# Forgetting attention: the cumulated gates enter the logits by a product instead of a DMA into the keys

## The chip, the cores and the metric

One core of a Trainium2 chip runs one program. The metric is the device time of one execution in microseconds; here, the median of three runs. TensorE multiplies, VectorE and ScalarE work elementwise and reduce, GpSimd takes a part of the elementwise work, and SyncE issues most of the DMAs. Each engine works through its own instructions in order and waits on semaphores for the others.

## The reference, cut to what matters

The program computes two transformer blocks on 256 tokens of width 1024. The change lies in the first of four branches of the first block, an attention of 16 heads of 64 with forget gates. A logit of query t and key s is a scaled product plus the difference of the cumulated log gates; a softmax over the keys up to t follows.

```python
fq = rms(heads(proj("fox_q"), 16), fox_q_norm_g)
fk = rms(heads(proj("fox_k"), 16), fox_k_norm_g)
log_f = log_sigmoid(proj("fox_f") + b_forget)          # one per token and head
cum_f = cumsum(log_f, axis=-1)
logits = einsum('bhqd,bhkd->bhqk', q, k) * scale + (cum_f[..., :, None] - cum_f[..., None, :])
logits = where(k_pos <= q_pos, logits, -inf)
y = softmax(logits) @ v
```

The term of the query is the same for all keys of a row, so the softmax removes it; only minus cum_f of the key is needed.

## The kernel before, in words

Activations lie feature by token: 8 tiles of 128 features by 256 tokens. A projection multiplies a unit of 128 x 1024 weights by the activations. To keep fp32 accuracy with the faster fp32r products, each unit and each activation is split into a high and a low part (`split`, line 357 on ScalarE for the high part, line 360 on VectorE or GpSimd for the low one), and three products of eight steps are summed (`mm3`; all products are at line 370). `unit` fetches weights by SyncE DMAs ahead of use, in one fixed order for the whole program.

`fox` is the branch of the change. It first projects the 16 forget gates (`st<-hh,wff`, 16 columns), takes their log sigmoid, and cumulates them along the tokens into `ncf`, 16 rows by 256 tokens, which holds minus cum_f with one head in each partition. Then four passes follow, each over a pair of head tiles (f and f+1, so four heads): a step for the queries, a step for the keys, a step for the values and the first two heads, and a step for the other two heads. `norm` copies a projection (`hraw`), squares it (`hsq`), sums the squares of each head by a product with a block matrix (`st<-hsq,cb`), takes the inverse root by Newton steps on VectorE (`nv`, `nr`, `nt`, 128x512 each), and scales twice. One of the scaled tiles has zeros in partitions 64 to 127 and the other in 0 to 63, since the gain is zero there (`fqg`, `fkg`), so a full product of 128 rows gives the logits of one head.

The zero half leaves a spare partition in each: 64 in the first tile, 0 in the second. Before the change it carries the gates. GpSimd writes ones into that row of the queries (line 909), and a DMA from ScalarE's queue copies the head's row of `ncf` into that row of the keys (line 915), four DMAs in a pass. The product of queries and keys then adds minus cum_f of the key by itself.

`fox_head` computes the logits of one head in a PSUM tile (`lg`): 128 queries by the first 128 keys, and the other 128 queries by all 256 keys. A VectorE instruction adds the mask and finds the maximum (line 933), ScalarE takes the exponential with its sum, VectorE divides (`fs`, line 367), TensorE transposes three tiles (`pt`, line 942), and ScalarE copies them out (`fp`). `av_pair` multiplies two heads with the values (`av`).

What sets the order: the program is written as generators. The passes of `fox` are woven one step at a time with the second branch's gated products (`branch(1, ...)`), and behind the last of them comes the next attention (`stick`). The modulation sums (`adacc`) run on VectorE as filler at a lower priority. From the written order and these priorities a planner lays down a fixed list for each engine: it simulates the engines with costs of its own, and at each point an engine takes the instruction of highest priority whose inputs are due by then. At run time each list is worked through in order. The PSUM tiles of the attention come from a pool of four, handed out in written order.

Of the kernel before, what the change touches and what calls it, by code (L numbers as in the profile page):

```python
# [18 lines left out]
P = 128  # L19
# [249 lines left out]
def flat(t):  # L269
    return t.rearrange("p f n -> p (f n)")  # L270
# [51 lines left out]
class Builder:  # L322
# [339 lines left out]
    def block1(self, xt, ct, fill):  # L662
        nc = self.nc
        with self.pool("b1") as bp, self.phase("b1t", t1=4, t2=6):
# [45 lines left out]
            yf = newy()  # L710
            fox = self.fox(h, yf, bp)
            step(fox, 3)
            weave((fox, 1), (self.branch(1, h, yl, acc, False), 1))
            ys = newy()
            stick = self.stick(h, ys, bp)
# [154 lines left out]
    def fox(self, h, y, bp):  # L870
        nc = self.nc

        ps = self.st()
        wf = self.wff
        n = 0
        for x, w in ((h[0], wf[0]), (h[1], wf[0]), (h[0], wf[1])):
            for k in range(KT):
                self.mm(ps[:16, :T], w[:, k * 16:(k + 1) * 16], x[:, k], start=n == 0, stop=n == 23)
                n += 1
        z, e = self.t("fz", rows=16), self.t("fe", rows=16)  # L880
        ncf = bp.tile([16, T], F32, tag="ncf", name="ncf")
        self.act(z, ps[:16, :T], AF.Identity, bias=self.pvc("bf")[:16])
        self.softplus_abs(e, z)

        self.ts(z, z, 0.0, None, ALU.min)
        self.tt(e, e, z, ALU.subtract)
        nc.vector.tensor_tensor_scan(out=ncf, data0=self.ones_t[:16], data1=e, initial=0.0, op0=ALU.mult,
                                     op1=ALU.add)
        cm = self.cst("cmask")
        rows = ((0, P), (P, 384))  # L890

        def norm(ps, tag, g):
            raw, sq = self.t("hraw", 512), self.t("hsq", 512)
            self.act(raw, ps)
            self.act(sq, ps, AF.Square)
            st = self.st()
            self.mm(st, self.cst("b64"), sq)
            r = self.rsqrt(st, 512, 64)
            out = [bp.tile([P, 2, T], F32, tag=f"{tag}{i}", name=f"{tag}{i}", bufs=2) for i in range(2)]
            for i in range(2):  # L900
                self.stt(flat(out[i]), raw, g[:, i:i + 1], r, ALU.mult, ALU.mult)
            return out


        spare = (64, 0)
        for f in range(0, KT, 2):
            qz = norm(self.pair("foxq", f, h), "qz", self.fqg)
            for i, row in enumerate(spare):
                nc.gpsimd.memset(qz[i][row:row + 1], 1.0)
            yield  # L910
            kz = norm(self.pair("foxk", f, h), "kz", self.pvs("fkg"))
            for i, row in enumerate(spare):
                for j in range(2):
                    hd = 2 * (f + j) + i
                    nc.scalar.dma_start(kz[i][row:row + 1, j], ncf[hd:hd + 1])
            yield
            v = bp.tile([P, 2, T], F32, tag="av", name="fv", bufs=2)
            self.act(v, self.tok("foxv", f // 2, h))
            for j in range(2):
                pts = [self.fox_head(qz[i][:, j], kz[i][:, j], cm, rows) for i in range(2)]  # L920
                self.av_pair(y, f + j, v, j, pts)
                yield

    def fox_head(self, q, k, cm, rows):
        nc = self.nc
        lg = self.ps("lg")
        self.mm(lg[:, 0:P], q[:, 0:P], k[:, 0:P])
        self.mm(lg[:, P:384], q[:, P:], k)

        s = self.t("fs", 384)  # L930
        nm, sm = self.col("fnm", 2), self.col("fsm", 2)
        for qt, (a, b) in enumerate(rows):
            nc.vector.tensor_tensor_reduce(out=s[:, a:b], in0=lg[:, a:b], in1=cm[:, T - (b - a):], scale=-1.0,
                                           scalar=3e38, op0=ALU.add, op1=ALU.min, accum_out=nm[:, qt:qt + 1])
            self.act(s[:, a:b], s[:, a:b], AF.Exp, scale=-1.0, bias=nm[:, qt:qt + 1], accum_out=sm[:, qt:qt + 1])
        nc.vector.reciprocal(sm, sm)
        pt = self.ps("pt")
        for qt, (a, b) in enumerate(rows):
            self.ts(s[:, a:b], s[:, a:b], sm[:, qt:qt + 1], None, ALU.mult)
            for j, c in enumerate(range(a, b, P)):  # L940
                o = T if j else qt * P
                nc.tensor.transpose(pt[:, o:o + P], s[:, c:c + P], self.cst("ident"))
        p = self.t("fp", 384)
        self.act(p, pt[:, :384])
        return p
# [688 lines left out]
```

## Time and profile before

| | us |
|---|---|
| median of 3 runs | 3097.9 |
| runs, lowest and highest | 3092.52 and 3099.93 |
| the profiled execution | 3095.87 |
| its span in the trace | 3094.1 |
| TensorE products busy | 2809.3 |
| VectorE busy | 2152.1 |
| ScalarE busy | 1344.0 |
| GpSimd busy | 851.9 |

The profile is of one execution. The span runs from the first to the last instruction in the trace; the 1.8 us to the profiled execution's time lie around it. PE is TensorE's products and PEld its weight loads, which lie under the products; DVE is VectorE, ACT ScalarE, POOL GpSimd and SP SyncE; ACTq is ScalarE's queue issuing a DMA. A group names what is written and what is read by the program's names, as `lg<-kz,qz` for the logits from keys and queries. "Idle before" is how long the engine did nothing ahead of an instruction, with what ended it; "issue" means that nothing the trace shows ended it.

### The profile page before, as it was taken

Reading aid. Unit: us, or ns where it says so; the run is one execution under the profiler, and the core shown is the slowest. Engines: PE = TensorE matmul, PEld = TensorE weight load, DVE = VectorE, ACT = ScalarE, POOL = GpSimd, SP = SyncE. Lnnn points to the kernel's source line nnn. Section 1 sums busy time; section 2 is a strip of 40 time slices with the busy share of each in tenths; the row PEclk is TensorE's granted clock in tenths of the full one; section 3 lists DMA queues with packets and bytes.
Section 4 is the critical chain, followed back from the end, with each engine's and each line's share of the span. In section 5 each row is a group of like instructions: output and inputs, shape, how many; then the busy total and the mean of one; then the engine's idle time right before and its main releaser. Section 6 shows DMA issues by size and latency. Waiting matters only on the chain. (4 is left out here: it accounts for less than half of the span.)

```text
span 3094.1 us, 49653 instructions
## 1 busy us (share of the span) xinstructions
PE 2809.3 (91%) x19760; PEld 2635.7 (85%) x19760; DVE 2152.1 (70%) x3412; ACT 1344.0 (43%) x2047; POOL 851.9 (28%) x643
## 2 busy tenths in 40 slices
PE   7997889988799887898999998999999999999898
PEld 6897778888799886798899988999998888888898
DVE  7599764679974899957699348868844499321554
ACT  5474446533344544345645554445434332111443
POOL 3243322243324434542102105444520111100000
PEclk9999999998899998999999999999999999999999
DMA  5345333466547555687656986654743223344353
GB/s 201 138 164 179 114 105 132 146 214 214 192 148 266 200 190 188 214 309 284 240 206 244 333 318 235 248 202 156 281 157 123 97 96 109 120 150 153 123 179 108
DMA packets 153416, 578.18 MB, mean 187 GB/s; under 512 B 17628, under 2 KB 17756, under 8 KB 146656
## 3 DMA queue, kind: packets, MB, share of 16 engines
q1 hardware_dynamic: 152496, 574.45, 52.1%
q8 instruction: 155, 2.54, 0.3%
q10 hardware_dynamic: 688, 0.56, 0.1%
q14 instruction: 77, 0.63, 0.1%
HBM read 516.73 MB, written 58.20 MB: 186 GB/s over the span
## 5 line engine op out<-in xcount | busy, mean ns | idle before, releaser
L357 ACT ACTIVATE whi<-raw 128x1024 fp32r<-128x1024 f32 (+1 forms) x650 | 675.7, 1045 | 747.4 <-PE mm L370 397.8
L360 POOL TENSOR_TENSOR wlo<-raw,whi 128x1024 fp32r<-128x1024 f32 (+1 forms) x248 | 647.0, 2613 | 1010.3 <-ACT whi L357 721.2
L360 DVE TENSOR_TENSOR wlo<-raw,whi 128x1024 fp32r<-128x1024 f32 (+1 forms) x293 | 382.8, 1307 | 242.3 <-ACT whi L357 231.0
L370 PE MATMUL mm<-hh,whi 128*128 128x256 f32 x3184 | 485.7, 294 | 33.1 <-DVE cv L360 19.2
L370 PE MATMUL mm<-hh,wlo 128*128 128x256 f32 x3184 | 469.3, 290 | 19.7 <-DVE wlo L360 17.6
L370 PE MATMUL mm<-hl,whi 128*128 128x256 f32 x3184 | 475.3, 292 | 0.0
L370 PEld LDWEIGHTS mm<-hh,whi 128*128 128x128 f32 x3184 | 431.2, 198 | 46.8 <-DVE cv L360 20.9
L370 PEld LDWEIGHTS mm<-hh,wlo 128*128 128x128 f32 x3184 | 426.0, 197 | 23.2 <-DVE wlo L360 18.8
L370 PEld LDWEIGHTS mm<-hl,whi 128*128 128x128 f32 x3184 | 431.7, 200 | 4.3 <-issue 3.6
L363 DVE SCALAR_TENSOR_TENSOR ca<-yp,pv,ca 128x256 f32<-128x256 f32 x720 | 357.2, 557 | 2.2
L370 PE MATMUL mm<-h,raw 128*128 128x256 f32 x1184 | 267.1, 379 | 0.0
L370 PEld LDWEIGHTS mm<-h,raw 128*128 128x128 f32 x1184 | 222.7, 190 | 29.5 <-issue 0.4
L363 DVE SCALAR_TENSOR_TENSOR adacc<-wada,sc,adacc 128x1024 f32<-128x1024 f32 x140 | 229.9, 1659 | 7.2 <-DMA wada<-in_wa 6.8
L360 POOL TENSOR_TENSOR gF<-cum 128x128 f32<-128x128 f32 x192 | 98.2, 542 | 337.2 <-DVE cum L1192 171.3
L370 PE MATMUL mm<-yh,whi 128*128 128x256 f32 x896 | 139.7, 295 | 23.1 <-ACT yh L357 16.3
L370 PEld LDWEIGHTS mm<-yh,whi 128*128 128x128 f32 x896 | 122.6, 199 | 30.1 <-ACT yh L357 20.6
L363 DVE SCALAR_TENSOR_TENSOR gt<-gt,mm 128x256 f32<-128x256 f32 x72 | 29.9, 416 | 161.7 <-ACT gt L357 161.6
L370 PE MATMUL mm<-yh,wlo 128*128 128x256 f32 x896 | 133.2, 290 | 2.8 <-DVE wlo L360 2.8
L370 PE MATMUL mm<-yl,whi 128*128 128x256 f32 x896 | 133.0, 290 | 2.6 <-DVE yl L363 2.1
L370 PEld LDWEIGHTS mm<-yh,wlo 128*128 128x128 f32 x896 | 120.0, 197 | 4.4 <-DVE wlo L360 3.2
L370 PEld LDWEIGHTS mm<-yl,whi 128*128 128x128 f32 x896 | 120.2, 197 | 3.6 <-DVE yl L363 2.7
L370 PE MATMUL mm<-y,raw 128*128 128x256 f32 x512 | 116.5, 384 | 0.0
(289 smaller groups left out, 4069.2 us busy)
## 6 DMA issues: line engine op xcount, KB each, us to landing
raw<-in_ws SPq DMA_DIRECT2D x744, 512.0 KB, 3.8
lo<-wlo SPq DMA_DIRECT2D x109, 512.0 KB, 3.0
wlo<-lo SPq DMA_DIRECT2D x109, 512.0 KB, 3.6
wada<-in_wa SPq DMA_DIRECT2D x48, 1024.0 KB, 4.9
raw<-in_ws SPq DMA_DIRECT2D x32, 384.0 KB, 3.0
memt<-in_tok SPq DMA_DIRECT2D x4, 256.0 KB, 4.6
xt<-in_tok SPq DMA_DIRECT2D x1, 1024.0 KB, 6.8
ct<-in_tok SPq DMA_DIRECT2D x1, 1024.0 KB
```

The costliest lines, as they stand in the source:

```text
L357: return self.nc.scalar.activation(out, in_, f, **k)
L360: return (eng or self.nc.vector).tensor_tensor(out=out, in0=a, in1=b, op=op)
L363: return self.nc.vector.scalar_tensor_tensor(out=out, in0=a, scalar=s, in1=b, op0=op0, op1=op1)
L370: return self.nc.tensor.matmul(out, lhsT=l, rhs=r, start=start, stop=stop, **k)
```

## The change

The ones row of the queries and the gate row of the keys are no longer written: the eight memsets and the sixteen DMAs are gone, and `norm`'s tiles are used as they are. `fox_head` gets `ncf` and the head's number instead. Ahead of each of its two logits products it adds one more product into the same PSUM columns: the stationary operand is the head's column of a 16 x 16 identity, repeated over 128 columns by a step of zero, and the moving operand is `ncf`, 16 rows by 128 or 256 tokens. That product writes the head's row of `ncf` to all 128 queries, and the product of queries and keys is summed on top.

```diff
--- before.py
+++ after.py
@@ -901,31 +901,27 @@
                 self.stt(flat(out[i]), raw, g[:, i:i + 1], r, ALU.mult, ALU.mult)
             return out
 
-
-        spare = (64, 0)
         for f in range(0, KT, 2):
             qz = norm(self.pair("foxq", f, h), "qz", self.fqg)
-            for i, row in enumerate(spare):
-                nc.gpsimd.memset(qz[i][row:row + 1], 1.0)
             yield
             kz = norm(self.pair("foxk", f, h), "kz", self.pvs("fkg"))
-            for i, row in enumerate(spare):
-                for j in range(2):
-                    hd = 2 * (f + j) + i
-                    nc.scalar.dma_start(kz[i][row:row + 1, j], ncf[hd:hd + 1])
             yield
             v = bp.tile([P, 2, T], F32, tag="av", name="fv", bufs=2)
             self.act(v, self.tok("foxv", f // 2, h))
             for j in range(2):
-                pts = [self.fox_head(qz[i][:, j], kz[i][:, j], cm, rows) for i in range(2)]
+                pts = [self.fox_head(qz[i][:, j], kz[i][:, j], ncf, 2 * (f + j) + i, cm, rows) for i in range(2)]
                 self.av_pair(y, f + j, v, j, pts)
                 yield
 
-    def fox_head(self, q, k, cm, rows):
+    def fox_head(self, q, k, ncf, hd, cm, rows):
         nc = self.nc
         lg = self.ps("lg")
-        self.mm(lg[:, 0:P], q[:, 0:P], k[:, 0:P])
-        self.mm(lg[:, P:384], q[:, P:], k)
+
+        pick = self.cst("ident")[:16, hd:hd + 1].to_broadcast([16, P])
+        self.mm(lg[:, 0:P], pick, ncf[:, 0:P], stop=False)
+        self.mm(lg[:, 0:P], q[:, 0:P], k[:, 0:P], start=False)
+        self.mm(lg[:, P:384], pick, ncf, stop=False)
+        self.mm(lg[:, P:384], q[:, P:], k, start=False)
 
         s = self.t("fs", 384)
         nm, sm = self.col("fnm", 2), self.col("fsm", 2)
```

## Rows read from the trace of the kernel before

**Rows 1.** The page, part 1: engine, busy us, share of the span, instructions.

```profile
PE 2809.3 (91%) x19760; PEld 2635.7 (85%) x19760; DVE 2152.1 (70%) x3412; ACT 1344.0 (43%) x2047; POOL 851.9 (28%) x643
```

**Rows 2.** Waits, 255 to 455 us: engine, line, releaser: total us, times, longest us.

```profile
PE lg L370 <- DMA kz<-ncf: 25.0, 4, 7.7
...
POOL qz L909 <- DVE qz L363: 14.0, 4, 5.8
...
PE pt L942 <- DVE fs L367: 7.7, 6, 1.8
```

**Rows 3.** Timeline, the four waits: start us, us, engine, line, instructions, [idle before].

```profile
276.16 1.42 DVE L363 SCALAR_TENSOR_TENSOR kz<-hraw,pv,nr 128x512 f32<-128x512 f32 x2
276.94 2.79 ACTq L915 DMA_DIRECT2D kz<-ncf  x4
...
280.53 1.62 PE L370 MATMUL lg<-kz,qz 128*128 128x128 f32 x4 [6.74 <-DMA kz<-ncf]
...
334.34 2.43 ACTq L915 DMA_DIRECT2D kz<-ncf  x4
...
336.61 1.62 PE L370 MATMUL lg<-kz,qz 128*128 128x128 f32 x4 [6.14 <-DMA kz<-ncf]
...
382.19 2.43 ACTq L915 DMA_DIRECT2D kz<-ncf  x4
...
383.94 1.02 PE L370 MATMUL lg<-kz,qz 128*128 128x128 f32 x4 [4.49 <-DMA kz<-ncf]
...
429.21 2.44 ACTq L915 DMA_DIRECT2D kz<-ncf  x4
...
432.45 1.62 PE L370 MATMUL lg<-kz,qz 128*128 128x128 f32 x4 [7.65 <-DMA kz<-ncf]
```

**Rows 4.** Timeline, VectorE and GpSimd ahead of the first and third wait.

```profile
255.67 1.22 DVE L360 TENSOR_TENSOR wlo<-raw,whi 128x1024 fp32r<-128x1024 f32 x1
...
260.74 3.56 DVE L363 SCALAR_TENSOR_TENSOR qz<-hraw,fqgs,nr 128x512 f32<-128x512 f32 x2
...
264.83 3.49 DVE L360 TENSOR_TENSOR wlo<-raw,whi 128x1024 fp32r<-128x1024 f32 x1
264.86 2.38 POOL L360 TENSOR_TENSOR wlo<-raw,whi 128x1024 fp32r<-128x1024 f32 x1
...
270.04 2.89 DVE L363 SCALAR_TENSOR_TENSOR nr<-nt,nr 128x512 f32<-128x512 f32 x1
...
371.34 2.78 DVE L360 TENSOR_TENSOR nt<-nr 128x512 f32<-128x512 f32 x1
...
377.35 2.88 DVE L363 SCALAR_TENSOR_TENSOR nt<-nt,nv 128x512 f32<-128x512 f32 x1
```

**Rows 5.** Groups by form, TensorE, whole span: shapes, count | busy us, mean ns | idle before.

```profile
L370 PE MATMUL mm<-h,raw 128*128 128x256 f32 x1184 | 267.1, 379 | 0.0
...
L370 PE MATMUL lg<-kz,qz 128*128 128x256 f32 x32 | 11.1, 432 | 0.0
...
L370 PE MATMUL lg<-kz,qz 128*128 128x128 f32 x32 | 7.4, 317 | 25.0 <-DMA kz<-ncf 25.0
...
L370 PE MATMUL st<-hh,wffh 128*16 128x256 f32 x8 | 1.1, 278 | 0.0
```

**Rows 6.** Timeline, TensorE, from one head to the next.

```profile
288.78 0.33 PE L942 MATMUL pt<-cc,fs 128*128 128x128 f32 x1 [0.28 <-DVE fs L367]
...
288.94 0.39 PE L370 MATMUL lg<-kz,qz 128*128 128x128 f32 x2
...
289.17 0.38 PE L942 MATMUL pt<-cc,fs 128*128 128x128 f32 x2
```

**Rows 7.** Timeline, TensorE's weight loads, after the products with the values.

```profile
292.29 0.19 PEld L370 LDWEIGHTS av<-fp,fv 128*64 128x64 f32 x2 [0.16 <-issue]
...
292.86 0.20 PEld L942 LDWEIGHTS pt<-cc,fs 128*128 128x128 f32 x2 [0.39 <-issue]
```

**Rows 8.** Windows: us, busy us (count) of PE, PEld, DVE, ACT, POOL; PEclk; DMA; GB/s.

```profile
277.00:287.00 10.00, 6.47 (x33) 6.32 (x34) 8.44 (x13) 3.10 (x6) 1.94 (x1) 0.66 0.42 148
```

## The prediction

> **What bounds the kernel now.** I read the page's busy shares first: TensorE is busy for 91% of the span [rows 1]. An engine that full sets the end, so a microsecond taken from it or given to it anywhere in the middle reaches the end, unless it was idle there. The change touches only the forgetting attention, which lies between some 240 and 460 us, so everything below is about TensorE in that stretch.
>
> The waits of the stretch come next [rows 2]. TensorE's largest is the first logits product of each pair of head tiles on the DMA that writes the gate row into the keys: four waits, 25.0 us in all. The next is 7.7 us on the softmax rows, in six waits. GpSimd loses 14.0 us ahead of the memsets of the ones row. The 25.0 us look like what the change is to gain.
>
> The timeline shows what the four waits consist of [rows 3]. In the first, VectorE starts the two key tiles at 276.16, 1.42 us for both; ScalarE issues the four DMAs from 276.94 on, for 2.79 us; the product starts at 280.53, after 6.74 us of idle time. So only the part from 276.94 on belongs to the DMA, 3.59 us, and the 3.15 us before it are a wait for VectorE that no edit of the change removes. The same difference, product start less start of the DMA issue, is 2.27, 1.75 and 3.24 us in the other three. Together the DMA has 10.85 of the 25.0 us; some 14.2 us are VectorE's.
>
> Why does TensorE arrive too early at all? The kernel's order on each engine is fixed ahead by a planner which puts an instruction where it expects its inputs. The product stands in the middle of a run of projections, which shows that it was placed by its due time. VectorE is what comes late [rows 4]. A split of a weight tile takes 1.22 us on VectorE at 255.67 and 3.49 us at 264.83, while GpSimd's split (264.86, 2.38 us) runs; two scalings of 128x512 take 3.56 us at 260.74, against 1.42 for the two of the keys in rows 3; a Newton step at 270.04 takes 2.89, against 0.71 for one of those. The excess is 2.27 + 2.14 + 2.18 = 6.6 us, and the first wait is 6.74 us. Before the third wait two steps of 2.78 and 2.88 us exceed 0.71 by 4.2 us, and that wait is 4.49 us. I read from this that the planner's place for the product is right but for the slowing of VectorE, and so that it already allows for the DMA about what the DMA takes.
>
> **The change part by part.** *DMAs and memsets go.* Sixteen DMAs of 1 KB leave ScalarE's queue and eight one-row memsets leave GpSimd. If the product kept its place among TensorE's instructions, each of the four waits would end when VectorE has written the first key tile: 10.85 us less. But the planner has no DMA to allow for any more and can put the product earlier by the same allowance. Work that stood before the product, and filled that time, then stands behind it. The period of one pair is the time from the key projection to the product, which gets shorter by the DMA, plus TensorE's work from the product to the next key projection, which gets longer by what was moved. Between the ends, 10.85 us of gain and none, I take none, by rows 4; 3 us would be what is left if the allowance were two thirds of the measured time.
>
> *The products added.* Each of 16 heads gets two: the same columns as its logits (128 and 256), with 16 rows of contraction instead of 128, and a stationary operand that repeats one column. Every fp32 product is two instructions here (64 logits instructions for 16 heads and two products) [rows 5]. A dense fp32 instruction of 256 columns costs 267.1 / 1184 = 0.226 us, and I take half, 0.113, for 128. A head costs 2 x (0.226 + 0.113) = 0.68 us, 16 heads 10.8 us. The upper end is the busy time of the present logits instructions with their tails and slow clock, 11.1 + 7.4 = 18.5 us. The lower end is the nearest row with a small operand: the forget gate's products with 16 columns, 1.1 us for eight of 256 columns, 0.14 us each with its tail; 64 instructions at half that for 32 of them make 6.7 us. I take 10.8, since the shape streamed is that of the logits. No row shows a product of 16 contraction rows. The Trainium skill ("TensorE: Matmul & The Clock Gate", section "Why this matters for your kernels") states that one matmul over 32 rows takes as long as one over 128; by it the sum would be the same 10.8 us, and no run here shows it yet.
>
> *What hides them.* Almost nothing. Heads follow each other tightly: the logits of the next head stand between the transposes of the last one (one transpose, two logits instructions, two transposes, then the rest of the logits) [rows 6]; so the next head's PSUM tile is taken only once the last head's transposes have begun, and its added products land there, in dense work. Only the first head of each pair can run its added products ahead of the keys, early, where TensorE is filled with projections too. All 10.8 us lie on TensorE's path. The logits of a head are ready 0.68 us later for VectorE, which has TensorE's projections as cover.
>
> *ScalarE and GpSimd freed.* ScalarE's next weight conversion is queued behind the four DMAs, which wait for the keys; GpSimd's next split stands behind the memsets, which wait for the scaled queries. Both start earlier. Who waits for them is TensorE's weights, and in rows 2 no wait of TensorE on them is as large as those shown. I cost this at nothing; the ends are 2.2 us of VectorE's slowing per split that moves into the key chain, 8.8 us for four, and as much of a gain where one moves out.
>
> *Clock.* After a wait TensorE runs slow: over 277 to 287 us the granted clock is 0.66 [rows 8], so part of it is at the 1.2 GHz level, after 6.74 us without work. At most 3.4 us per wait are lost so, 13.6 in all, and less, because the clock is low while there is nothing to run too. With waits as long as before it stays; I take 0, with up to half of it back where the waits shrink.
>
> The sum: 0 + 10.8 + 0 + 0 = +10.8 us on the profiled execution, 3095.9, makes 3106.7. That execution is 2.0 us below the median of the three runs, 3097.9; put on the median, the sum gives 3108.7. The forecast, between the two, is 3108.
>
> **The rivals.** *A, the waits shrink by the DMA.* The product stays where it is, 10.85 us go, the added products bring 10.8, and the sum is 0: 3096 to 3098. With half of the clock's loss back it is -6.8 us, 3091. For it: 10.85 us are measured. Against it: the planner places by due time, rows 4. It decides where the planner's allowance for the DMA is below 1 us or so.
>
> *B, TensorE empties at each change of height.* Going from 128 rows to 16 and back, the next weights aren't loaded under the running product. The row for it is the exit from the 64-column products with the values: the load of the next transpose sits idle for 0.39 us [rows 7]. Against it: the forget gate's 16-column products, eight in 1.1 us, have no such gap around them in rows 5. With two visits to the small shape per head, 32 visits at some 0.24 us (a half of 0.39, rounded up for the entry) are 7.7 us more: 3116. The upper end, 0.39 at every visit, is 12.5, 3121. The Trainium skill ("TensorEngine Tiling (Array Packing)", section "Tiling Modes", under "Key Properties") says that a change of tiling mode drains TensorE; the trace agrees for the 64-column products and not for the 16-column ones.
>
> *C, freed splits lengthen the key chain.* ScalarE converts during the chain, GpSimd splits during it, and VectorE slows four times by 2.2 us: +8.8 on top, 3117. It decides from the first GpSimd split that overlaps a Newton step of the keys more than now.
>
> *D, the new order dissolves the waits.* With other places for projections and splits TensorE has work until the keys are there: 25.0 us less, the clock's loss partly back, 10.8 more: -14 to -20, 3078 to 3084. Nothing in the profile speaks for it but that the order is made anew. That the change doesn't do what it says is no case: DMA and memsets can't remain.
>
> **How the numbers follow.** Forecast 0.42, A 0.20 (half of it with the clock back), B 0.20, C 0.10, D 0.08. What a measurement here can tell from no change is 0.3%, 9.3 us: 3088.6 to 3107.2. The forecast's own range is 3103 to 3116 by the bounds of the added products; a third of it is within 0.3%. Slower: 0.28 + 0.18 + 0.08, less a little for a gain elsewhere, 0.50. Faster: D and a part of A, 0.16. Same: the rest, 0.34. The range leaves out D and the far end of B and C: 3088 to 3121.
>
> **What would show it.** Right: the wait of TensorE at the first logits product of a pair is still there, four times, with VectorE's key tile as its releaser and together 18 to 26 us long; 64 new product instructions cost about 10 us of TensorE; the stretch from the forget gate's products to the last head ends some 10 us later. Wrong: the four waits sum to 15 us or less (A or D); loads with idle time beside the added products (B); longer waits and GpSimd splits inside the key chain (C). The prediction fails most simply if the planner allowed less for the DMA than it takes.

## The result, and the profile after

The changed kernel takes 3116.18 us (median of six runs, 3110.14 to 3123.13), before 3095.24 in runs beside it. The ratio is 1.0065, with a 95% interval of 1.0047 to 1.0083: 20 us slower. The forecast was 3108, slower by 10 to 13. The profiled execution of after took 3122.5 us, 6 us above its median, so of the difference of the two traces the last few microseconds are that execution's own.

The page, part 1, with its span:

```profile
span 3120.7 us, 49737 instructions
...
PE 2836.5 (91%) x19824; PEld 2648.1 (85%) x19824; DVE 2154.4 (69%) x3412; ACT 1342.3 (43%) x2047; POOL 841.6 (27%) x635
```

TensorE has 64 instructions more and 27.2 us more of busy time than in [rows 1]; VectorE and ScalarE have what they had. GpSimd has lost the eight memsets.

TensorE's waits in the same part of the work (255 to 480 us; columns as in [rows 2]):

```profile
PE lg L370 <- DVE kz L363: 17.7, 4, 6.0
PE pt L938 <- DVE fs L367: 5.5, 5, 1.4
PE mm L370 <- DVE wlo L360: 2.5, 1, 2.5
```

The four waits at the first logits product of a pass are still there, now for VectorE's key tile, and 17.7 us long in place of the 25.0 of [rows 2]. The timeline has them one by one, to be read beside [rows 3]:

```profile
279.76 0.80 PE L370 MATMUL lg<-kz,qz 128*128 128x128 f32 x2 [6.04 <-DVE kz L363]
280.49 1.22 PE L370 MATMUL lg<-ncf,cc 16*128 16x256 f32 x2
281.64 1.22 PE L370 MATMUL lg<-kz,qz 128*128 128x256 f32 x2
282.30 1.20 PE L370 MATMUL mm<-hh,whi 128*128 128x256 f32 x3
...
334.37 0.80 PE L370 MATMUL lg<-kz,qz 128*128 128x128 f32 x2 [3.61 <-DVE kz L363]
...
390.44 0.52 PE L370 MATMUL lg<-kz,qz 128*128 128x128 f32 x2 [2.28 <-DVE kz L363]
...
443.01 0.80 PE L370 MATMUL lg<-kz,qz 128*128 128x128 f32 x2 [5.74 <-DVE kz L363]
```

The first pass of after gets its keys 0.77 us earlier than before (279.76 against 280.53), the last 10.56 us later (443.01 against 432.45). So the loss grows pass by pass, in what TensorE does between the waits. From one head to the next, the timeline of after, to be read beside [rows 6]:

```profile
287.27 0.27 PE L938 MATMUL pt<-cc,fs 128*128 128x128 f32 x1
287.47 0.48 PE L370 MATMUL lg<-ncf,cc 16*128 16x128 f32 x2
287.88 0.44 PE L938 MATMUL pt<-cc,fs 128*128 128x128 f32 x2
288.16 0.39 PE L370 MATMUL lg<-kz,qz 128*128 128x128 f32 x2
288.47 0.69 PE L370 MATMUL lg<-ncf,cc 16*128 16x256 f32 x2
289.10 0.70 PE L370 MATMUL lg<-kz,qz 128*128 128x256 f32 x2
289.44 0.94 PE L370 MATMUL mm<-yl,whi 128*128 128x256 f32 x5
```

The same stretch of the kernel before ends here, as does the first head's:

```profile
281.59 1.63 PE L370 MATMUL mm<-hl,whi 128*128 128x256 f32 x5
...
289.63 0.94 PE L370 MATMUL mm<-hh,whi 128*128 128x256 f32 x5
```

From the first transpose to the next projection before took 289.63 - 288.78 = 0.85 us and after takes 289.44 - 287.27 = 2.17: 1.32 us more, where the prediction had 0.68. The weight loads of the same stretch show why:

```profile
287.47 0.29 PEld L370 LDWEIGHTS lg<-ncf,cc 16*128 16x128 f32 x2 [0.16 <-issue]
287.88 0.20 PEld L938 LDWEIGHTS pt<-cc,fs 128*128 128x128 f32 x2
288.05 0.30 PEld L370 LDWEIGHTS lg<-kz,qz 128*128 128x128 f32 x2
288.47 0.29 PEld L370 LDWEIGHTS lg<-ncf,cc 16*128 16x128 f32 x2
289.10 0.30 PEld L370 LDWEIGHTS lg<-kz,qz 128*128 128x128 f32 x2 [0.33 <-issue]
```

A load normally begins some 0.1 us ahead of its product, under the product before it, as at 288.05 for the product at 288.16. At each change between 16 and 128 rows, load and product begin together (287.47, 287.88, 288.47 and 289.10 in both fences), and the load sits idle before that, for up to 0.33 us. After a wait TensorE runs at the lower of its two levels, 1.2 GHz: from 443 to 447 us the granted clock is 0.50. There loads, products and the idle time before the loads are longer (the last row is that window: its us, TensorE's busy us and instructions, the granted clock, the DMA's share, GB/s):

```profile
443.74 0.50 PEld L370 LDWEIGHTS lg<-ncf,cc 16*128 16x128 f32 x2 [0.22 <-issue]
444.88 0.50 PEld L370 LDWEIGHTS lg<-kz,qz 128*128 128x128 f32 x2 [0.65 <-issue]
...
443.00:447.00 4.00, 3.99 (x12) 0.50 0.45 183
```

**The sum from the trace.** Of four heads in a pass, the first costs its early product (0.41 us) and 282.30 - 279.76 = 2.54 us, against 281.59 - 280.53 = 1.06 before: 1.9 more. Two cost 1.32 more; the one that meets the products with the values costs some 1.1 more by the same reading (in the second pass 347.69 to 351.49 us in after, 344.82 to 347.47 before). That is 4 x (1.9 + 2 x 1.32 + 1.1) = 22.6 us of products, less 7.3 us of waits: 15.3. A milestone behind the branch is the first instruction of the next attention on ScalarE, the absolute value of `z`; it begins at 457.6 us before and 474.2 after, 16.6 later. The rest arises behind that: at the first modulation sum (`adas`, 577.9 and 598.5) the distance is 20.6 us.

### The profile page after: what moved, and what is told of

The parts are those of the page before. It is cut to its first block, busy times and chain, and to the rows that moved or that the text cites. A ratio compares the mean times of both kernels' runs of the same rounds, so it can differ in the third digit from the quotient of the medians.

```text
span 3120.7 us, 49737 instructions
## 1 busy us (share of the span) xinstructions
PE 2836.5 (91%) x19824; PEld 2648.1 (85%) x19824; DVE 2154.4 (69%) x3412; ACT 1342.3 (43%) x2047; POOL 841.6 (27%) x635
## 3 DMA queue, kind: packets, MB, share of 16 engines
q8 instruction: 155, 2.54, 0.3%
## 5 line engine op out<-in xcount | busy, mean ns | idle before, releaser
L370 PEld LDWEIGHTS mm<-hh,wlo 128*128 128x128 f32 x3184 | 426.6, 197 | 22.7 <-DVE wlo L360 18.7
```

What stands on the lines that cost most here:

```text
L370: return self.nc.tensor.matmul(out, lhsT=l, rhs=r, start=start, stop=stop, **k)
```

## The experiments

Two theories of the products' price were set against each other: H, TensorE empties at each change of height between 16 and 128 rows; and O, the products cost that much by themselves. The waits were a separate question: what is the DMA's part worth, and why is VectorE late at all? "Milestone" is the first `se<-z` of each trace, 457.6 us before and 474.2 after.

**No DMA, no memsets, no products.**

```diff
-        pick = self.cst("ident")[:16, hd:hd + 1].to_broadcast([16, P])
-        self.mm(lg[:, 0:P], pick, ncf[:, 0:P], stop=False)
-        self.mm(lg[:, 0:P], q[:, 0:P], k[:, 0:P], start=False)
-        self.mm(lg[:, P:384], pick, ncf, stop=False)
-        self.mm(lg[:, P:384], q[:, P:], k, start=False)
+        self.mm(lg[:, 0:P], q[:, 0:P], k[:, 0:P])
+        self.mm(lg[:, P:384], q[:, P:], k)
```

> The changed kernel without its added products: neither DMA, memsets nor products, so the gates are left out of the logits. It measures what taking the DMA and the memsets away is worth by itself. The forecast's step (the planner moves the product up by the DMA's time) expects nothing: 3095 us, 0 against before. Rival A (the waits shrink by the DMA's 10.85 us, part of the clock's loss comes back) expects 3079 to 3084. The trace of after shows four waits of 17.7 us in place of 25.0, 7.3 us less; if that reading is whole, 3088.

Measured: 3091.31 us, 0.9985 of before (0.9972 to 0.9999), so 4.6 us less. The milestone is at 449.7, 7.8 us earlier. TensorE's waits in this kernel:

```profile
PE lg L370 <- DVE kz L363: 17.4, 4, 5.8
```

The forecast's 0 lies just outside the interval and rival A's 14 to 19 us far outside; the 7.3 us read from the trace of after lie within it. 7.6 us of waits go, the branch ends 7.8 us earlier, and 4 of these are lost again by the first `adas` (574.1 against 577.9, 3.8 earlier); "Left open" below says why. After stands 24.4 us behind this kernel there (598.5 against 574.1), which is the products' price by this pair.

**The products alone, beside the DMA.** The kernel before, with `fox_head` as after.

> The kernel before with the added products beside the DMA and the memsets, so the gates are added twice. It measures the products by themselves, with the waits of before in place. If the sum of after is two separate terms (23.2 us of products, 7.3 us of waits gone), this gives 23 us over before: 3118, above after. If the products run in the time of the waits, it is at most 3107.

Measured: 3119.06 us, 1.0074 (1.0056 to 1.0091): 23 us, as two separate terms would have it. The waits are 23.9 us long, nearly those of [rows 2], with the DMA as their releaser, so the products don't run in their time. At the first `adas` the products cost 22.5 us by this pair (600.4 against 577.9). TensorE's waits for the keys:

```profile
PE lg L370 <- DMA kz<-ncf: 23.9, 4, 10.9
```

**The products 128 rows high.**

```diff
-        ncf = bp.tile([16, T], F32, tag="ncf", name="ncf")
+        ncf = bp.tile([P, T], F32, tag="ncf", name="ncf")
+        nc.gpsimd.memset(ncf, 0.0)
...
-        pick = self.cst("ident")[:16, hd:hd + 1].to_broadcast([16, P])
+        pick = self.cst("ident")[:, hd:hd + 1].to_broadcast([P, P])
```

> The changed kernel with the added products made 128 rows high: the gates' tile has 128 partitions, zero from 16 on, and the repeated column of the identity has 128 rows. Same products, columns and order. Theory H (TensorE empties at each change between 16 and 128 rows) expects a dense cost of 0.68 us per head in place of some 1.35, 10 us less than after: 3106, and no idle loads at the added products. Theory O (the products cost that much by themselves: repeated column, longer sums in one bank, their place) expects 3116 as after.

Measured: 3100.57 us, 1.0007 (0.9994 to 1.0020). Eight times the rows, and 0.6% less time than after. The milestone is at 458.95, 15.2 us earlier than in after. The timeline of its TensorE from one head to the next, to be read beside that of after:

```profile
286.65 0.27 PE L939 MATMUL pt<-cc,fs 128*128 128x128 f32 x1
286.76 0.39 PE L370 MATMUL lg<-ncf,cc 128*128 128x128 f32 x2
286.98 0.38 PE L939 MATMUL pt<-cc,fs 128*128 128x128 f32 x2
287.20 0.39 PE L370 MATMUL lg<-kz,qz 128*128 128x128 f32 x2
287.42 0.60 PE L370 MATMUL lg<-ncf,cc 128*128 128x256 f32 x2
287.86 0.59 PE L370 MATMUL lg<-kz,qz 128*128 128x256 f32 x2
288.10 0.94 PE L370 MATMUL mm<-yl,whi 128*128 128x256 f32 x5
```

The stretch takes 288.10 - 286.65 = 1.45 us, 0.60 more than before and 0.72 less than after, in the same order. No load in it is idle. H holds, O falls: a visit to the small shape costs 0.72 / 2 = 0.36 us, and the added products by themselves 0.60 us a head. Against the kernel without products this one is 9.3 us slower by the medians, 9.2 at the milestone and 10.7 at the first `adas` (584.8 against 574.1): so much do the sixteen heads' products cost at full height.

**One product of 384 columns.** The gates' tile holds the first 128 tokens twice, so one 16-row product covers both logits products.

```diff
...
-        self.mm(lg[:, 0:P], pick, ncf[:, 0:P], stop=False)
-        self.mm(lg[:, 0:P], q[:, 0:P], k[:, 0:P], start=False)
-        self.mm(lg[:, P:384], pick, ncf, stop=False)
-        self.mm(lg[:, P:384], q[:, P:], k, start=False)
+        self.mm(lg[:, 0:384], pick, ncf, stop=False, skip_group_check=True)
+        self.mm(lg[:, 0:P], q[:, 0:P], k[:, 0:P], start=False, skip_group_check=True)
+        self.mm(lg[:, P:384], q[:, P:], k, start=False, skip_group_check=True)
```

> The changed kernel with one added product of 16 rows by 384 columns per head in place of two of 128 and 256: the gates' tile holds the first 128 tokens twice. Same columns, half of the changes of height, and for the first head of a pair all of it stands ahead of the keys. Theory H expects 12 heads at some 0.3 us less and four first heads at some 1.2 us less: 8 us less than after, 3108. Theory O expects only the four first heads' part, 5 us: 3111.

Measured: 3108.85 us, 1.0037 (1.0024 to 1.0050), by H's figure; its interval holds O's 3111 too, so it separates less than the run with 128 rows. The milestone is at 465.1, about halfway between after and the kernel with 128 rows.

**Both mends.** 128 rows, and one product of 384 columns.

> Both mends together: one added product per head, 384 columns, 128 rows high. Theory H expects no change of height to be left, so only the first heads' products that now stand ahead of the keys come off the kernel with 128 rows (some 0.5 to 1 us at the low clock for each of four): 3097 to 3100. Theory O, by which half the products would be half the cost, expects 3096 or less.

Measured: 3105.83 us, 1.0026 (1.0014 to 1.0038), 6 us above the upper end of what was expected. The trace doesn't show it: the milestone is at 458.3 and the first `adas` at 584.2, against 458.95 and 584.8 with two products. The branch takes the same, so a single product of the same columns gains nothing there; why the medians differ by 5 us is open.

**Products of 64 rows.** As the 128-row edit, with 64 partitions.

> The changed kernel with added products of 64 rows in place of 16 (the gates' tile has 64 partitions, zero from 16 on). If every change of height empties TensorE, this is as after: 3116. If only heights below 64 do, it is as with 128 rows: 3101.

Measured: 3119.85 us, 1.0072 (1.0049 to 1.0096): as after. The loads are idle at the same places and as long:

```profile
287.94 0.29 PEld L370 LDWEIGHTS lg<-ncf,cc 64*128 64x128 f32 x2 [0.16 <-issue]
...
289.57 0.30 PEld L370 LDWEIGHTS lg<-kz,qz 128*128 128x128 f32 x2 [0.33 <-issue]
```

**The memsets back on GpSimd.**

```diff
             qz = norm(self.pair("foxq", f, h), "qz", self.fqg)
+            for i, row in enumerate((64, 0)):
+                nc.gpsimd.memset(qz[i][row:row + 1], 1.0)
```

> The changed kernel with the eight memsets of the ones rows put back on GpSimd (they meet a zero in the keys, so nothing else changes). Rival C (GpSimd, freed of the memsets, splits inside the key chain and slows VectorE) expects 4 to 9 us less than after: 3107 to 3112. The forecast, which costed GpSimd's release at nothing, expects 3116, within 3 us.

Measured: 3120.00 us, 1.0070 (1.0049 to 1.0091), as after. The interval alone leaves room for a few microseconds; the trace has the milestone at 473.3 and the first `adas` at 597.6, 0.9 us ahead of after in both, where rival C expects 4 to 9. Rival C falls.

**Early DMA.** The kernel before, with two sets of query and key tiles that are kept through the branch, their zeros and ones written once, `norm` writing only the 64 partitions of a tile's own head, and the DMAs ahead of the query projection.

```diff
             for i in range(2):
-                self.stt(flat(out[i]), raw, g[:, i:i + 1], r, ALU.mult, ALU.mult)
+                h = slice(64 * i, 64 * i + 64)
+                self.stt(flat(out[i])[h], raw[h], g[h, i:i + 1], r[h], ALU.mult, ALU.mult)
...
         for f in range(0, KT, 2):
-            qz = norm(self.pair("foxq", f, h), "qz", self.fqg)
-            for i, row in enumerate(spare):
-                nc.gpsimd.memset(qz[i][row:row + 1], 1.0)
-            yield
-            kz = norm(self.pair("foxk", f, h), "kz", self.pvs("fkg"))
+            qz, kz = kept[f // 2 % 2]
             for i, row in enumerate(spare):
                 for j in range(2):
                     hd = 2 * (f + j) + i
                     nc.scalar.dma_start(kz[i][row:row + 1, j], ncf[hd:hd + 1])
+            norm(self.pair("foxq", f, h), qz, self.fqg)
+            yield
+            norm(self.pair("foxk", f, h), kz, self.pvs("fkg"))
```

> The kernel before with its gate rows kept, but written early: the query and key tiles of two passes are kept through the branch, zeros and ones are written once, the norm scales the 64 partitions of its heads alone, and the DMAs of the gate rows stand ahead of the query projection of their pass, so no product waits for them. No added products. If the DMA's time is worth what the kernel without products showed (-4.6 us), this gives 3093 or a little less (24 fewer steps on GpSimd and VectorE are not on the path). If the waits were really the DMA's (rival A), it gives 3079 to 3084.

Measured: 3091.39 us, 0.9972 (0.9961 to 0.9983). It gains 6 to 9 us, as the kernel without products did, and computes all. So that gain is to be had without a single product. The waits that are left, 19.1 us in place of 25.0, three on VectorE and one without a releaser in the trace:

```profile
PE lg L370 <- DVE kz L363: 13.8, 3, 6.4
PE lg L370 <- issue: 5.3, 1, 5.3
```

**All splits of the branch on VectorE.** The kernel before; `lo_pool` gives GpSimd's share of the low halves.

```diff
+            self.lo_pool = (0, 1)
             step(fox, 3)
             weave((fox, 1), (self.branch(1, h, yl, acc, False), 1))
+            self.lo_pool = LO["b1t"]
```

> The kernel before with all weight splits of the forgetting attention's part on VectorE, none on GpSimd. The reading of the waits (VectorE late because GpSimd's splits slow it, by 6.6 us ahead of the first wait) expects the four waits of TensorE to fall from 25.0 us to the DMA's part, about 11 us, and the time to 3084 to 3090. If VectorE is late because it has too much work, the waits stay at 25 us or grow, and the time is 3098 or more.

Measured: 3065.83 us, 0.9892 (0.9874 to 0.9910), 31 us less, more than expected. TensorE's waits in it:

```profile
PE lg L370 <- DMA kz<-ncf: 4.1, 3, 3.2
```

The Newton steps by form, 240 to 430 us, first of the kernel before:

```profile
L363 DVE SCALAR_TENSOR_TENSOR nt<-nt,nv 128x512 f32<-128x512 f32 x16 | 19.5, 1219 | 0.3
...
L360 POOL TENSOR_TENSOR wlo<-raw,whi 128x1024 fp32r<-128x1024 f32 x21 | 56.3, 2683 | 108.2 <-ACT whi L357 71.6 <-PE mm L370 28.5 <-DVE fnm L933 8.0
```

and then of this one:

```profile
L360 DVE TENSOR_TENSOR wlo<-raw,whi 128x1024 fp32r<-128x1024 f32 x44 | 54.9, 1248 | 6.1 <-ACT whi L357 2.9 <-ACT fp L357 1.8 <-PE mm L370 1.2
L363 DVE SCALAR_TENSOR_TENSOR nt<-nt,nv 128x512 f32<-128x512 f32 x16 | 10.9, 684 | 0.1
...
L360 POOL TENSOR_TENSOR wlo<-raw,whi 128x1024 fp32r<-128x1024 f32 x4 | 11.5, 2870 | 48.7 <-ACT whi L357 45.1 <-PE mm L370 3.6
```

A step falls from 1219 ns to 684 on average once GpSimd splits only four weight tiles there instead of 21. The mean hides two kinds: before, twelve of the sixteen steps take 0.68 to 0.69 us and four, each during a split on GpSimd, 2.78 to 2.88. The same holds beyond these steps: in the trace of before, all 20 VectorE instructions between 255 and 455 us that took over 0.3 us more than the shortest of their form ran during a split on GpSimd, and their excess is 38.9 us in all, some 1.9 us for each of its 21 splits there; not every instruction that met a split is among them. A split on VectorE takes it 1.25 us; so moving a split over shortens VectorE's chain although its work grows. The milestone comes at 429.6, 28 us earlier. The edit also makes the planned order anew, and this run doesn't separate what that does.

**The same splits, with early DMA, and with the change.**

> The kernel with early gate DMAs, and all weight splits of the forgetting attention's part on VectorE. If the two gains are about separate parts of the same waits (6 us for the DMA, 31 us for GpSimd's slowing), and the second has left 4.1 us of waits on the DMA, this gives 3060 to 3063. If the early DMA's gain needs the long waits, 3066 as without it.

Measured: 3067.89 us, 0.9899 (0.9874 to 0.9923): no further gain. With the keys in time, there is no wait for an early DMA to shorten.

> The changed kernel with the same splits on VectorE. If the products cost 23 us wherever the waits are, this gives 3066 + 23 - 4 = 3085, 19 us over before with those splits. If the changed kernel lost only because the waits stayed, it gives 3062 to 3066.

Measured: 3092.26 us, 0.9983 (0.9968 to 0.9998). Beside 0.9892 without the change it loses 0.9%, some 28 us. That is above the 19 us expected; the interval of the difference reaches from some 21 to 35 us. At the first `adas` it stands 22.7 us behind (568.9 against 546.2). The products cost about as much where there is next to no wait (3.9 us, one).

**Splits on VectorE to the end of the mixers.** As the kernel with early DMA and VectorE's splits, without setting `lo_pool` back.

> As the kernel with early gate DMAs and splits on VectorE, and the splits stay on VectorE through the next attention and to the end of the first block's mixers. If GpSimd slows VectorE's chains there too, another 3 to 10 us come off: 3052 to 3058. If VectorE then has too much to do (it has the modulation sums there), it gives 3065 or more.

Measured: 3048.55 us, 0.9838 (0.9812 to 0.9865), the fastest of all: some 50 us less than before by the ratio, and a little more gain than expected.

## Why the prediction was right or wrong

**What bounds the kernel: right.** TensorE's path sets the end. Its 22.6 us of products less 7.3 us of waits, 15.3, appear as 16.6 us at the milestone and as 20 us at the end.

**"I take none" for the DMA's part of the waits: wrong, by 7.3 us.** The step that failed is the one which read from [rows 4] that the planner already allows for the DMA about what it takes. What it allowed can be counted on TensorE's list, as the projection instructions between the sum of squares of a pass's keys (`st<-hsq,cb`) and its first logits product on the keys. The four passes, first before and then after (window, us, TensorE's busy us on projections (count), granted clock, DMA share, GB/s):

```profile
254.00:280.50 26.50, 18.13 (x145) 0.97 0.47 172
315.70:336.60 20.90, 14.77 (x120) 0.92 0.36 130
366.90:383.90 17.00, 12.55 (x102) 1.00 0.36 128
413.50:432.40 18.90, 11.29 (x91) 0.91 0.35 123
...
253.40:279.70 26.30, 17.53 (x139) 0.97 0.49 175
317.40:334.30 16.90, 13.02 (x104) 0.95 0.36 126
377.10:390.40 13.30, 10.65 (x86) 1.00 0.40 138
428.00:443.00 15.00, 8.92 (x70) 0.97 0.29 97
```

Of 458 instructions 59 were moved behind the product. At the 0.12 us that one takes these are 7.1 us, where the DMA had 10.85: the allowance was two thirds of it, the case for which the prediction had 3 us left. That accounts for 10.85 - 7.1 = 3.8 of the 7.3 us. Another 1.7 are the four early added products, which run on TensorE ahead of the wait and shorten it; 0.8 is a longer wait for a weight tile in the first pass (2.5 against 1.7), 0.7 that VectorE's first key tiles are done sooner after the sum, counted over the four passes, and 0.3 remains. The first pass alone would mislead. Only six instructions, 0.7 us, were moved there against 3.59 us of DMA, and yet the wait shrank by no more than 0.70, since VectorE begins the first key tile 2.81 us later than in [rows 3], behind six modulation sums from 255 us on in place of three:

```profile
278.97 1.40 DVE L363 SCALAR_TENSOR_TENSOR kz<-hraw,pv,nr 128x512 f32<-128x512 f32 x2
```

Why the planner puts them there is open. Rival A had all 10.85 us; the truth, 7.3 to 7.6 in two kernels, lies between.

**Why VectorE is late: right.** The excess on VectorE while GpSimd splits was read as the cause of the remaining 14.2 us. Without GpSimd's splits there the waits fall from 25.0 to 4.1 us. The run expected the DMA's 11 us to stay; they went too, so once VectorE is in time, the planner's place for the product covers most of the DMA. That GpSimd's splits slow VectorE is shown by the steps themselves; that all 31 us come from it is argued, since the order changed with the splits.

**10.8 us of products: right for their shape, wrong for their height.** With 128 rows a head costs 0.60 us by the timeline, against 0.68 costed, and the kernel with them stands 9.2 to 10.7 us behind the one without products, against 10.8. With 16 rows it costs 1.32, and 1.9 at the low clock after a wait. The term was sized at half, because changes of height were put at nothing. That is rival B, which had 7.7 us more and 12.5 at its upper end; measured are 22.6 - 10.8 = 11.8 by the sum, near the upper end, and 13.7 to 15.2 us between after and the kernel with 128 rows (first `adas`, milestone), beyond it. Its price per visit was 0.24 to 0.39 us, measured 0.36 at a granted clock of 1.00 (287 to 290 us). Its time, 3116, is the measured one, but only since 12 us of emptying and 7 us of shorter waits partly cancel. The forecast's 3108 is nearer than its mechanism for the same reason: its two errors have opposite signs, which is luck. Its argument against B, the forget gate's 16-column products in [rows 5], was about columns, and says nothing of rows; those are also fp32r products, one instruction each, where the added ones are two.

By the Trainium skill ("TensorEngine Tiling (Array Packing)", section "Tiling Modes", under "Key Properties") a change of tiling mode drains TensorE. The traces agree for 16 and 64 rows (loads idle for 0.16 and 0.33 us in both, 0.36 us for a visit at 16), and not for the 16 columns of the forget gate. What the skill says of a short contraction ("TensorE: Matmul & The Clock Gate", "Why this matters for your kernels"), that it takes as long as a full one, agrees with the shortest instructions of the trace of after, 270 ns among the added ones of 16 rows and 275 among the logits of 128. The medians, 373 and 379, mix two shapes and the slow clock. Shortest, median and longest in ns:

```profile
L370 PE MATMUL lg<-ncf,cc x64: 270/373/791, 258.2 to 462.8; 16*128 16x128 f32 x32, 16*128 16x256 f32 x32
...
L370 PE MATMUL lg<-kz,qz x64: 275/379/796, 279.8 to 463.4; 128*128 128x128 f32 x32, 128*128 128x256 f32 x32
```

**What hides them: right, but for 1.7 us.** Only the first head's first product ran ahead of the keys (258.23 in the trace of after), and these four shorten the waits behind them. At the first `adas` the products alone cost 24.4, 22.5 and 22.7 us in three pairs of kernels: with neither DMA nor memsets, beside the old waits, and where there is next to no wait.

**ScalarE and GpSimd at nothing: right** for GpSimd, by the run with the memsets. ScalarE's release from the DMAs wasn't tried by itself.

**Clock at nothing:** not separated. The products after a wait run at the low level (granted 0.50 from 443 to 447 us), which is in their 1.9 us.

**The signs.** The waits are there, four times, on VectorE's key tile, but their 17.7 us lie just below the 18 to 26 named as right. The added products cost about twice the 10 us, and the idle loads beside them, the sign of B, are there.

**Left open.** Between the milestone and the first `adas` after is 4.0 us longer than before, and so are the kernel without products (4.1) and the one with the DMA kept (4.4). Most of it is order: between the forget gate and the first product of the next attention (456.70 and 472.97 us) TensorE has 1122 projection instructions before and 1104 in after and in these two, so 18 of 0.12 us, 2.2, stand behind the milestone in place of ahead; and six products with the values (0.8 us) stand ahead of it that before has behind it. TensorE's waits for `se` up to the first `adas` are 2.5 us longer (4.7 against 2.2). That makes 3.9 for after. So of these three kernels' distances to the one before at the milestone, some 1.4 us are order. Why the planner sets these orders is open.

## What to carry to other kernels

A wait that names a DMA has to be split at the moment the DMA was issued: what lies before that is another engine's delay, and where the order is planned ahead, even the DMA's own part doesn't come back whole: here work worth 7.1 of its 10.85 us went behind the product. A small product among large ones should have the height of its neighbours: here 128 rows, 112 of them zeros, cost 0.60 us a head and 16 rows 1.32, 0.36 us more a visit. Ask first why the producer is late: here moving GpSimd's splits to VectorE was worth 31 to 50 us, against 6 to 9 for the best way to save the DMA.

## What the hardware showed unexpectedly

Products of 64 rows leave the loads idle as those of 16 do (0.16 us on entering, 0.33 on leaving, in both), so between these two the size of the change doesn't matter. The forget gate's 16 columns show next to no gap (0.2 us ahead of eight loads, before), though the 64 columns of the products with the values do (0.39 us in [rows 7]); what decides between these is open. An engine that helps can slow the one it helps: a VectorE step of 0.68 us took 2.78 to 2.88 in four of sixteen cases, all during a split on GpSimd, and a split given to GpSimd cost VectorE more (some 1.9 us) than doing it (1.25 us).
